# Tree attention on one core: SyncE's store of heads 88 and 90 in eleven pieces in place of four

## The chip, the core and the metric

The kernel runs on one core of a Trainium2 chip. Five engines work side by side: TensorE (PE, with its weight loads as PEld) multiplies matrices, VectorE (DVE), ScalarE (ACT) and GpSimd (POOL) work on tiles, and SyncE (SP) only issues transfers and waits. Sixteen DMA engines move data between the chip's memory (HBM) and the on-chip buffer. A transfer is issued by SP, ACT or POOL; the profile lists the packets of each issuer under a queue of its own: q1 is SP's, q10 ACT's, q0 POOL's.

The metric is the device time of one execution in microseconds. It is longer than the profile's span, which goes from the first instruction to the last.

## The reference

Q, K and V have 8 x 12 = 96 heads of 512 positions by 64 numbers, in fp32. The positions are the nodes of a binary tree, and a node attends to itself and to its ancestors:

```python
for i in range(seq):
    mask[i, i] = 1
    parent = i
    while parent > 0:
        parent = (parent - 1) // 2
        mask[i, parent] = 1
scores = np.einsum('bhqd,bhkd->bhqk', Q, K) * scale
scores = scores + (1 - mask) * (-1e9)
weights = np.exp(scores - np.max(scores, axis=-1, keepdims=True))
weights = weights / (np.sum(weights, axis=-1, keepdims=True) + 1e-10)
return np.einsum('bhqk,bhkd->bhqd', weights, V)
```

## The kernel before

The 96 heads are worked off as 48 pairs, `i` = 0 to 47 (`NP` = 48). For each pair the kernel transposes Q and K on TensorE (`narrow_k`, `wide_k` and their like, lines 401 and 433), makes the scores (`scores1`, `scores2`, lines 458 to 501; the mask enters as a product of small codes), takes their exponential on ScalarE (lines 476 and 507), multiplies by V (`values`, line 551) and divides by the sum that a column of ones in V gives (`norm`: a reciprocal on line 581 and a product on line 583, both on VectorE). From the ninth pair on the heads of a pair stand two apart: `head(i, a)` makes pair 44 out of heads 88 and 90, pair 45 out of 89 and 91, pair 46 out of 92 and 94, pair 47 out of 93 and 95.

The results lie in tiles of eight heads, one row of a tile for each of the 128 partitions; one row of one head is 1 KB. `store` (line 592) writes `n` heads, or the rows `p0` to `p1` of them, with one DMA. POOL issues nearly all loads and, eight heads at a time, the stores of heads 0 to 75 and 80 to 87, in the order that `pool_program` lists. SP issues two loads at the start, the store of heads 76 to 79 (`store_apart`), and then, from the loop's last three rounds and behind the loop, the stores of the last eight heads:

- in round 45 (`NP - 3`) heads 88 and 90, cut by rows at the places in `edges`: 4, 8, 12 and 104 rows,
- in round 46 heads 89 and 91, in round 47 heads 92 and 94, each in one DMA of 128 rows,
- behind the loop head 93; head 95 goes out from ACT.

An engine's instructions run in the order in which they are written, so SP issues these one after the other; each store waits for the product on line 583 that fills its tile. The framework also gives the DMAs of SP and ACT eight completion counters, one after another and then again from the first. A DMA that takes a counter for the second time first waits until the DMA that had the counter before has landed. In the kernel before, the store of 104 rows, those of heads 89 and 91, 92 and 94, and head 93 take the counters of the four loads at the start, and head 95's takes that of heads 76 to 79.

At the end SP waits for every counter (under line 792 in the profile, line 793 in the changed kernel), and a barrier over all engines closes the program.

Of the kernel before, what the change touches and what calls it, by code (L numbers as in the profile page):

```python
# [119 lines left out]
def kernel(  # L120
# [9 lines left out]
    P = nc.NUM_PARTITIONS  # L130
# [4 lines left out]
    NP = 2 * NQ  # L135
# [128 lines left out]
    def head(i, a):  # L264

        return 2 * i + a if i < WIDE else 4 * (i // 2) + i % 2 + 2 * a
# [178 lines left out]
    def turn(name, i):  # L445
        heads = [head(i + b, a) for b in range(2 if i >= WIDE else 1) for a in range(2)]
        assert all((name, h) in issued for h in heads), (name, i)
        {"kst": (narrow_k, wide_k), "qst": (narrow_q, wide_q)}[name][i >= WIDE](i)
        return i + (2 if i >= WIDE else 1)
# [4 lines left out]
    def scores1(i):  # L454

        sp = psS.tile([P, 2, 512], fp32, name="s1")
        for a in range(2):
            nc.tensor.matmul(  # L458
                out=sp[:, a, :],
                lhsT=(k1code if i < WIDE else k1wide)[64 * a:64 * a + CODE_ROWS, :],  # L460
                rhs=(q1code[64 * a:64 * a + CODE_ROWS, :] if i < WIDE
                     else q1wide[64 * a:64 * a + CODE_ROWS, :, :]),
                start=True, stop=False,
            )
        for a in range(2):
            nc.tensor.matmul(  # L466
                out=sp[:, a, :], lhsT=keys(i, a, TOP),
                rhs=qTs[i][64 * a:64 * a + 64, :, :].rearrange("p t c -> p (t c)"),
                start=False, stop=True,
            )  # L470
        et = etpool.tile([P, 2, 4, 128], bf16, name="e1")
        nc.scalar.activation(  # L472
            out=et[:, :, :, :].rearrange("p a t c -> p (a t c)"),
            in_=sp[:, :, :].rearrange("p a c -> p (a c)"),
            func=AF.Exp, scale=scale,
        ) if i < WIDE else nc.scalar.activation(  # L476
            out=et[:, :, :, :].rearrange("p a t (r u) -> p a (t r) u", u=2),
            in_=sp[:, :, :].rearrange("p a (u c) -> p a c u", u=2),
            func=AF.Exp, scale=scale,
        )  # L480
        ets[i] = et
# [31 lines left out]
    def scores2(i):  # L513
        if i >= WIDE:
            return scores2_wide(i)
        sp = psS.tile([P, 2, 4, 128], fp32, name="s2")
        flat = sp[:, :, :, :].rearrange("p a t c -> p a (t c)")
        for a in range(2):
            nc.tensor.matmul(
                out=sp[:, a, :, 32:128], lhsT=k2code[64 * a:64 * a + CODE_ROWS, :],  # L520
                rhs=q2code[64 * a:64 * a + CODE_ROWS, :].rearrange(
                    "p (t c) -> p t c", t=4
                )[:, :, 32:128],
                start=True, stop=False,
            )
        for t, lo, hi in ((2, 32, 192), (0, 192, 256), (3, 288, 448), (1, 448, 512)):
            for a in range(2):
                nc.tensor.matmul(
                    out=flat[:, a, lo:hi], lhsT=keys(i, a, TILE2[t]),
                    rhs=qTs[i][64 * a:64 * a + 64, :, :].rearrange("p t c -> p (t c)")[:, lo:hi],  # L530
                    start=False, stop=t == 1, skip_group_check=t in (2, 3),
                )
        nc.scalar.activation(
            out=e2s[i % NE][:, :, :, 32:128].rearrange("p a t c -> p (a t) c"),
            in_=sp[:, :, :, 32:128].rearrange("p a t c -> p (a t) c"),
            func=AF.Exp, scale=scale,
        )

    def values(i):

        if i < NP - 1:
            obs[i] = ob = psO.tile([P, 2, 512], fp32, name="ob")
        else:
            obs[i] = ob = psS.tile([P, 2, 512], fp32, name="s1")
        e1, e2, vt = ets[i], e2s[i % NE], vts[(head(i, 0) // VB) % NV]

        vtile = VTILE if i < WIDE else WVTILE
        assert all(("vt", n, head(i, a)) in issued for n in PARTS[i >= WIDE] for a in range(2))

        def product(e, a, t, tile_v, lo=0, hi=128, **flags):  # L550
            nc.tensor.matmul(  # L551
                out=ob[lo:hi, a, 65 * t:65 * t + 65],
                lhsT=e[:, a, PLACE[t], lo:hi],
                rhs=vt[vtile[tile_v][0]][:, head(i, a) % VB, vtile[tile_v][1], 0:D + 1],
                **flags,
            )

        def halves(a):
            for t in (0, 1):
                product(e2, a, t, 1 + SELF[t], 0, 64, start=False, stop=t == 1)  # L560
                product(e2, a, t, 1 + t, 64, 128, start=False, stop=t == 1)

        for a in range(2):
            for t in range(4):
                product(e1, a, t, 0, start=t == 0, stop=False)
            for t in (2, 3):
                product(e2, a, t, 1 + t, start=False, stop=False)
            if i == NP - 1:
                halves(a)
        if i < NP - 1:  # L570
            for a in range(2):
                halves(a)

    def norm(i):
        g = head(i, 0) // VO
        if g not in ofs:
            ofs[g] = opool.tile([P, VO, 4, D], fp32, name="of")
        o4 = obs[i][:, :, 0:260].rearrange("p a (t c) -> p a t c", c=D + 1)
        rec = small.tile([P, 2, 4, 1], fp32, name="rec")
        for a, n in ((0, 2),) if i < NP - 1 else ((0, 1), (1, 1)):  # L580
            nc.vector.reciprocal(out=rec[:, a:a + n, :, :], in_=o4[:, a:a + n, :, D:D + 1])  # L581
            first, last, step = head(i, a) % VO, head(i, a + n - 1) % VO, head(i, 1) - head(i, 0)
            nc.vector.tensor_tensor(  # L583
                out=ofs[g][:, first:last + 1:step, :, :],
                in0=o4[:, a:a + n, :, 0:D],
                in1=rec[:, a:a + n, :, :].to_broadcast([P, n, 4, D]),
                op=ALU.mult,
            )
# [8 lines left out]
        )  # L597

    APART, APART_AT = 76, 41

    def store_apart():

        store(nc.sync, APART, 4)
# [92 lines left out]
    def spread_by(copy, table, steady, i):  # L696

        o, j = divmod(i, 8)
        todo = table.get(i, [])
        if 4 <= o + 1 < NH // VB:  # L700
            todo = todo + [(o + 1,) + piece for piece in steady.get(j, [])]
        for args in todo:
            spread(copy, *args)
# [8 lines left out]
    def spin(name, n):  # L712

        pool, shape = (psS, [P, 2, 512]) if name == "s1" else (psO, [P, 2, 512])
        tile = pool.tile(shape, fp32, name=name)
        for _ in range(n):
            nc.tensor.matmul(
                out=tile[:, 0, :], lhsT=idle[:, 0:128], rhs=idle[:, :], start=True, stop=True
            )
# [9 lines left out]
    for i in range(NP + 1):  # L729
        steps = FIRST[i] if i < len(FIRST) else "SVK" if i % 2 else "SVQ"  # L730
        for step in steps:
            if step == "S" and i < NP:
                scores1(i)
                scores2(i)
            if step == "V" and i >= 1:
                values(i - 1)
                norm(i - 1)
                valued = True
            if step == "K" and kdone < NP:
                kdone = turn("kst", kdone)  # L740
            if step == "Q" and qdone < NP:
                qdone = turn("qst", qdone)
            if step == "W":
                nc.scalar.copy(
                    out=codes[64:64 + CODE_ROWS, 1280:1536], in_=codes[0:CODE_ROWS, 1280:1536]
                )
            if step == "X":
                spin("s1" if valued else "ob", 2)
            if step == "D":
                spread_by(nc.vector.tensor_copy, BY_VECTOR, STEADY_VECTOR, i)  # L750
            if step == "A":
                spread_by(nc.scalar.copy, BY_SCALAR, {}, i)
        if "D" not in steps:
            spread_by(nc.vector.tensor_copy, BY_VECTOR, STEADY_VECTOR, i)
        if "A" not in steps:
            spread_by(nc.scalar.copy, BY_SCALAR, {}, i)
        pool(i)
        if i == APART_AT:
            store_apart()
        if i >= NP - 3 and i < NP:  # L760
            edges = (0, 4, 12, 24, P) if i == NP - 3 else (0, P)
            for p0, p1 in zip(edges, edges[1:]):
                store(nc.sync, head(i - 1, 0), 2, 2, p0, p1)
    assert not program
# [32 lines left out]
```

## Time and profile before

| | |
|---|---|
| median of 3 runs | 134.81 us (134.7 to 135.66) |
| the profiled execution's own time | 135.35 us |
| its span | 133.6 us |
| outside the span | 1.75 us |
| busy: PE / DVE / ACT / POOL | 113.8 / 100.4 / 94.4 / 73.2 us |
| moved by DMA | 32.26 MB, 242 GB/s on average |
| packets on SP's queue (q1) | 1831, of 1.83 MB |

The page gives shares over the whole span. The change concerns the last 11 us of it, so the rows that count are those of short windows there: SP's issues in order of time with the time that each took, the packets of each queue in a window, and for a transfer the time from its issue to its landing. For DMAs that are split over fewer than sixteen engines the view has no time to landing.

### The profile page before, as it was taken

Reading aid. Unit: us, or ns where it says so; the run is one execution under the profiler, and the core shown is the slowest. Engines: PE = TensorE matmul, PEld = TensorE weight load, DVE = VectorE, ACT = ScalarE, POOL = GpSimd, SP = SyncE. Lnnn points to the kernel's source line nnn. Section 1 sums busy time; section 2 is a strip of 40 time slices with the busy share of each in tenths; the row PEclk is TensorE's granted clock in tenths of the full one; section 3 lists DMA queues with packets and bytes.
Section 4 is the critical chain, followed back from the end, with each engine's and each line's share of the span. In section 5 each row is a group of like instructions: output and inputs, shape, how many; then the busy total and the mean of one; then the engine's idle time right before and its main releaser. Section 6 shows DMA issues by size and latency. Waiting matters only on the chain.

```text
span 133.6 us, 5522 instructions
## 1 busy us (share of the span) xinstructions
PE 113.8 (85%) x2414; PEld 79.2 (59%) x2417; DVE 100.4 (75%) x249; ACT 94.4 (71%) x153; POOL 73.2 (55%) x100
## 2 busy tenths in 40 slices
PE   6884999999799899989989699969989997989800
PEld 2352676667577577756757468747657765756500
DVE  3437769998999998979796699977887896674620
ACT  4358289979769778868858769859785975959600
POOL 6978725364374999986932799538089510002000
PEclk9999599999999999999999999999999999999985
DMA  4999999999999999999999999999999999999981
GB/s 136 207 173 193 197 200 199 202 201 207 202 199 203 202 204 205 201 205 201 205 204 201 318 251 201 295 271 250 322 221 335 224 321 400 402 397 405 366 301 38
DMA packets 32239, 32.26 MB, mean 242 GB/s; under 512 B 1199, under 2 KB 29487, under 8 KB 32215
## 3 DMA queue, kind: packets, MB, share of 16 engines
q0 software_dynamic: 29824, 29.63, 113.8%
q1 hardware_dynamic: 1831, 1.83, 4.0%
q10 hardware_dynamic: 560, 0.46, 1.1%
q8 instruction: 19, 0.31, 0.9%
q14 instruction: 5, 0.04, 0.1%
HBM read 37.94 MB, written 12.58 MB: 378 GB/s over the span
## 4 chain that ended last, share of the span: by engine, by line
DMA 48%; PE 33%; issue 6%; POOL 5%; DVE 2%; ACT 2%; DVEq 0%; ACTq 0%; POOLq 0%
DMA vst<-in_V_dram 33%; PE ob L551 11%; DMA kst<-in_K_dram 10%; DMA qst<-in_Q_dram 6%; PE s L458 5%; PE qtp L433 3%; PE ktp L401 3%; PE s L466 3%; PE s L501 3%; PE s L491 3%; POOL kst L239 2%; POOL qst L239 2%; POOL vst L239 1%; DVE of L583 1%; ACT e L507 1%
## 5 line engine op out<-in xcount | busy, mean ns | idle before, releaser
L476 ACT ACTIVATE e<-s 128x1024 bf16<-128x1024 f32 x40 | 41.0, 1024 | 21.0 <-PE s L466 20.4
L551 PE MATMUL ob<-vt,e 128*128 128x65 bf16 (+1 forms) x940 | 37.8, 198 | 3.5 <-DVE of L583 2.1
L551 PEld LDWEIGHTS <-e 128*128 128x128 bf16 (+1 forms) x960 | 30.7, 103 | 11.9 <-DVE of L583 2.1
L507 ACT ACTIVATE e<-s 128x384 bf16<-128x384 f32 x80 | 34.7, 490 | 0.0
L583 DVE TENSOR_TENSOR of<-ob,rec 128x512 f32<-128x512 f32 x47 | 32.5, 691 | 1.6
L336 POOL COPY vt<-vst 32x512 int32<-32x512 int32 (+1 forms) x32 | 24.3, 759 | 8.1 <-DVE vt L336 5.0
L336 DVE COPY vt<-vst 64x1024 bf16<-64x1024 bf16 (+6 forms) x42 | 18.5, 440 | 3.8 <-DMA vst<-in_V_dram 3.1
L458 PE MATMUL s<-codes 40*128 40x512 bf16 x96 | 19.7, 398 | 1.2 <-issue 0.4
L581 DVE RECIPROCAL rec<-ob 128x8 f32<-128x8 f32 x47 | 9.6, 205 | 14.2 <-PE ob L551 13.5
L466 PE MATMUL s<-kq 64*128 64x512 bf16 x96 | 18.8, 382 | 0.0
L592 POOL DMA_DIRECT2D out_dram<-of x11 | 9.9, 900 | 15.7 <-DVE of L583 13.2
L280 POOL DMA_DIRECT2D vst<-in_V_dram x15 | 11.0, 736 | 12.2 <-DMA vst<-in_V_dram 5.2
L501 PEld LDWEIGHTS <-kq 64*128 64x128 bf16 x320 | 12.6, 94 | 4.8 <-issue 0.3
L501 PE MATMUL s<-kq 64*128 64x160 bf16 (+1 forms) x320 | 15.1, 208 | 0.2 <-issue 0.2
L401 PE MATMUL ktp<-ptile,kst 128*64 128x128 bf16 x320 | 12.5, 219 | 2.3 <-issue 2.0
L491 PE MATMUL s<-codes 40*128 40x384 bf16 x80 | 13.9, 334 | 0.3
L441 DVE COPY kq<-qtp 128x1024 bf16<-128x1024 bf16 x20 | 13.6, 681 | 0.6 <-PE qtp L433 0.6
L433 PE MATMUL qtp<-ptile,qst 128*64 128x128 bf16 x320 | 12.7, 219 | 1.2 <-issue 1.2
L472 ACT ACTIVATE e<-s 128x1024 bf16<-128x1024 f32 x8 | 8.2, 1023 | 6.0 <-PE s L466 6.0
L251 POOL DMA_DIRECT2D qst<-in_Q_dram x13 | 9.5, 730 | 4.6 <-DMA kst<-in_K_dram 1.5
L251 POOL DMA_DIRECT2D kst<-in_K_dram x12 | 8.9, 745 | 5.3 <-DMA kst<-in_K_dram 1.5
L491 PEld LDWEIGHTS <-codes 40*128 40x128 bf16 x80 | 6.3, 94 | 8.9 <-issue 1.3
(42 smaller groups left out, 121.4 us busy)
## 6 DMA issues: line engine op xcount, KB each, us to landing
out_dram<-of POOLq DMA_DIRECT2D x10, 1024.0 KB, 15.9
kst<-in_K_dram POOLq DMA_DIRECT2D x8, 512.0 KB, 14.9
qst<-in_Q_dram POOLq DMA_DIRECT2D x7, 512.0 KB, 16.6
vst<-in_V_dram POOLq DMA_DIRECT2D x12, 256.0 KB, 14.1
vst<-in_V_dram POOLq DMA_DIRECT2D x6, 512.0 KB, 12.7
qst<-in_Q_dram POOLq DMA_DIRECT2D x8, 256.0 KB, 11.5
kst<-in_K_dram POOLq DMA_DIRECT2D x6, 256.0 KB, 11.5
out_dram<-of POOLq DMA_DIRECT2D x1, 512.0 KB, 20.6
```

What stands on the lines that cost most here:

```text
L251: return nc.gpsimd.dma_start(out=kept[b][:, h0 % KB:h0 % KB + n, :, :].rearrange("p (g x) t d -> p g (x t d)", x=2), in_=wide[:, h0 // 2:( ...
L336: return copy(out=dst, in_=src)
L401: nc.tensor.transpose(out=columns(kp[64 * a:64 * a + 64, :], mixed, (256, 2), (leaves - mixed, 2), (1, 32)), in_=st[:, 2 * i % KB // 2 + a ...
L433: nc.tensor.transpose(out=halves[64 * a:64 * a + 64, :, c:c + 64], in_=st[:, 2 * i % KB // 2 + a, 4 * u + t, :], identity=ptile[:, 0:128],)
L458: nc.tensor.matmul(out=sp[:, a, :], lhsT=(k1code if i < WIDE else k1wide)[64 * a:64 * a + CODE_ROWS, :], rhs=(q1code[64 * a:64 * a + CODE_ ...
L466: nc.tensor.matmul(out=sp[:, a, :], lhsT=keys(i, a, TOP), rhs=qTs[i][64 * a:64 * a + 64, :, :].rearrange("p t c -> p (t c)"), start=False, ...
L476: ) if i < WIDE else nc.scalar.activation(
L491: nc.tensor.matmul(out=flat[:, a, :, :].rearrange("p u (t c) -> p u t c", t=4)[:, :, :, 16:64], lhsT=k2wide[64 * a:64 * a + CODE_ROWS, :], ...
L501: nc.tensor.matmul(out=flat[:, a, :, lo:hi], lhsT=keys(i, a, WTILE2[t]), rhs=qT[64 * a:64 * a + 64, :, lo:hi], start=False, stop=t == 1, s ...
L507: nc.scalar.activation(out=e2s[i % NE][:, a, :, 32:128].rearrange("p t (r u) -> p t r u", u=2), in_=flat[:, a, :, :].rearrange("p u (t r) ...
L551: nc.tensor.matmul(out=ob[lo:hi, a, 65 * t:65 * t + 65], lhsT=e[:, a, PLACE[t], lo:hi], rhs=vt[vtile[tile_v][0]][:, head(i, a) % VB, vtile ...
L583: nc.vector.tensor_tensor(out=ofs[g][:, first:last + 1:step, :, :], in0=o4[:, a:a + n, :, 0:D], in1=rec[:, a:a + n, :, :].to_broadcast([P, ...
```

## The change

The rows of heads 88 and 90 are cut at eleven places in place of four. The pieces have 5, 6, 7, 8, 9, 10, 11, 13, 14, 15 and 30 rows, which is 128 rows as before, of two heads each. Nothing else is edited.

```diff
     APART, APART_AT = 76, 41
+    LAST_ROWS = (0, 5, 11, 18, 26, 35, 45, 56, 69, 83, 98, P)
 
     def store_apart():
...
         if i >= NP - 3 and i < NP:
-            edges = (0, 4, 12, 24, P) if i == NP - 3 else (0, P)
+            edges = LAST_ROWS if i == NP - 3 else (0, P)
             for p0, p1 in zip(edges, edges[1:]):
                 store(nc.sync, head(i - 1, 0), 2, 2, p0, p1)
```

In the built program the instructions of PE, DVE, ACT and POOL stand as before. SP issues seventeen DMAs in place of ten. The counters fall otherwise: the pieces of 8, 9, 10 and 11 rows take those of the four loads at the start, the piece of 13 rows that of heads 76 to 79. From there on a store waits for another piece: 14 rows for the landing of the 6 rows, 15 for the 7, 30 for the 8, heads 89 and 91 for the 9 rows, heads 92 and 94 for the 10, head 93 for the 11, and head 95 on ACT for the 5. The pieces of 6 and 7 rows wait for nothing, as those of 8 and 12 rows did before.

## The prediction

> **What bounds the kernel now.** I began with the stretch that the change touches, the end of the program, and read the busy time of each engine there, two microseconds to a row. The columns are busy times with counts, then the granted clock, the share of the sixteen DMA engines in use, and GB/s.
>
> ```profile
> 122.00:124.00 2.00, 1.90 (x36) 1.26 (x37) 0.78 (x3) 1.84 (x4) 0.00 (x0) 1.00 1.02 391
> ...
> 126.00:128.00 2.00, 0.38 (x10) 0.21 (x7) 1.29 (x5) 0.00 (x0) 0.00 (x0) 1.00 1.02 368
> 128.00:130.00 2.00, 0.00 (x0) 0.00 (x0) 0.00 (x0) 0.00 (x0) 0.00 (x0) 0.87 0.79 275
> 130.00:132.00 2.00, 0.00 (x0) 0.00 (x0) 0.00 (x0) 0.00 (x0) 0.00 (x0) 0.50 0.23 80
> 132.00:134.00 2.00, 0.00 (x0) 0.00 (x0) 0.00 (x0) 0.00 (x0) 0.00 (x0) 0.50 0.00 0
> ```
>
> Until 128 all DMA engines are full. From 128 on nothing computes; only transfers run, and from 130 on only a quarter of the DMA engines: a few late ones finish by themselves. So the end is set by DMAs. To see whose, I took the issues of the end in order of time, and the time from issue to landing. The first three lines are VectorE finishing pair 44, VectorE finishing the last head, and ACT's store of it; the fourth is POOL's last store.
>
> ```profile
> 121.54 0.69 DVE L583 TENSOR_TENSOR of<-ob,rec 128x512 f32<-128x512 f32 x1
> 127.18 0.42 DVE L583 TENSOR_TENSOR of<-s,rec 128x256 f32<-128x256 f32 x1
> 127.64 0.35 ACTq L592 DMA_DIRECT2D out_dram<-of  x1
> 120.43 0.90 POOL L592 DMA_DIRECT2D out_dram<-of  x1 [13.23 <-DVE of L583]
> ...
> out_dram<-of POOLq DMA_DIRECT2D x1, 1024.0 KB, 9.4
> out_dram<-of SPq DMA_DIRECT2D x1, 256.0 KB, 5.7
> out_dram<-of SPq DMA_DIRECT2D x1, 256.0 KB, 5.5
> out_dram<-of ACTq DMA_DIRECT2D x1, 128.0 KB, 4.9
> ```
>
> ACT's store lands at 127.64 + 4.9 = 132.5, and the span of 133.6 ends 1.1 us later, with the final waits and the barrier. POOL's store of 1 MB, issued at 120.43, has its last byte down at 120.43 + 9.4 = 129.8. What does SP's queue do meanwhile? Queue rows of three windows:
>
> ```profile
> q0 software_dynamic: 309, 1.16, 100.3%
> q8 instruction: 1, 0.02, 2.1%
> ...
> q0 software_dynamic: 93, 0.36, 86.3%
> q1 hardware_dynamic: 16, 0.01, 5.1%
> ...
> q1 hardware_dynamic: 256, 0.25, 70.7%
> q0 software_dynamic: 31, 0.11, 27.1%
> ```
>
> The first two lines are 122 to 124.95: q1 has no row at all, though SP issued from 122.26 on. The next two are 124.95 to 126, the last two 127 to 128. So a store of SP waits on each DMA engine behind what POOL had queued there, and its packets run between 125 and the end. A packet of q1 takes 70.7% of 16 engine-microseconds over 256, or 44 ns; a store of 256 KB is 16 packets on each engine, 0.70 us, and one of 128 KB 0.35.
>
> **The change, part by part.** All of it is on SP. Its issues after 122, start and duration:
>
> ```profile
> 122.26 0.29 SPq L592 DMA_DIRECT2D out_dram<-of  x1
> 122.59 1.10 SPq L592 DMA_DIRECT2D out_dram<-of  x1
> 123.73 1.12 SPq L592 DMA_DIRECT2D out_dram<-of  x1
> 124.89 0.37 SPq L592 DMA_DIRECT2D out_dram<-of  x1
> 125.37 0.39 SPq L592 DMA_DIRECT2D out_dram<-of  x1
> 126.19 0.39 SPq L592 DMA_DIRECT2D out_dram<-of  x1
> 127.09 0.35 SPq L592 DMA_DIRECT2D out_dram<-of  x1
> ```
>
> In order these are the pieces of 4, 8, 12 and 104 rows, then heads 89/91, 92/94 and 93. Pair 44 is ready at 121.54 + 0.69 = 122.23, SP starts at once, and the four pieces hold SP until 125.26. The store of heads 89/91 starts only then.
>
> *How the pieces are spread.* The page's q1 row tells:
>
> ```profile
> q1 hardware_dynamic: 1831, 1.83, 4.0%
> ```
>
> If every DMA has one packet per row and head and one more for each DMA engine that it uses, the other stores and loads of SP come to 272 + 50 + 528 + 272 + 272 + 144 = 1538, which leaves 293 = 256 + 37 for heads 88/90, and 37 = 4 + 8 + 12 + 13. So 4, 8 and 12 rows go to as many engines, one row each, and 104 rows go to 13 engines, eight each. By the same count the new pieces use 5, 6, 7, 8, 9, 10, 11, 13, 14, 15 and 15 engines, together 113; ten pieces have one row per engine, the last has two. The Trainium skill ("DMA: Bandwidth & Descriptors", on why a DMA increments its semaphore by 16) states this rule, the largest number up to 16 that divides the rows, and adds that the lowest-numbered engines are taken; the first half agrees with the 1831 packets, the second no row here shows.
>
> *What it can gain.* An engine that ends late ends earlier by each row that it no longer gets. Before, none has more than 1 + 1 + 1 + 8 = 11 rows, 22 packets, so 22 x 44 ns = 0.97 us is the most that can go, and only if the latest engine had all and now gets none. By the skill's rule of lowest numbers the thirteenth engine goes from 8 rows to 5, 0.26 us, and the first four from 11 to 12.
>
> *What the issues cost.* Seven more DMAs on SP, each at between 0.29 and 1.12 us plus 0.04 to the next (122.59 + 1.10 to 123.73). Which end? The pieces with several rows per engine took 0.37 to 0.39. Of the three with one row per engine two took 1.10 and 1.12, the first 0.29, but that one had stood waiting for VectorE for a long time. The extra is equal in both, so it does not look like a queue's chance delay, and the 104 rows behind them were fast under the same load. The nearest rows to the pieces of 6 to 15 rows are therefore those two, and I take 1.15 us from start to start for nine pieces (6, 7, 8, 9, 10, 11, 13, 14, 15), 0.33 for the first and 0.48 for the 30 rows (124.89 to 125.37). The other bound is 0.41 for all.
>
> *The sum.* Pieces start at 122.26 and 122.59; nine at 1.15 bring the 30 rows to 132.94, heads 89/91 to 133.42, 92/94 to 133.90 and head 93 to 134.38, in place of 127.09. The new waits for counters are met long before, since everything that a piece queues behind is down at 129.8. The DMA engines are then empty, so part of the delay is got back: no queue, only the transfer's own latency. For this the nearest row is a 256 KB load at the program's start, with little else in flight, which landed 3.0 us after its issue:
>
> ```profile
> firstK<-in_K_dram SPq DMA_DIRECT2D x1, 256.0 KB, 3.0
> ```
>
> Less its 0.70 of packets that is 2.3 us beside the packets, an upper bound, as three other loads ran with it. The lower bound is what ACT's store shows: issued at 127.64, no q10 row before 128, so at least 0.4. I take 1.3. The 40 packets of the three stores then end at 133.42 + 1.3 + 40 x 0.044 = 136.5, where 132.5 was: **4.0 us later**. Nothing covers this, since no engine computes after 127.6; POOL's stores, compute and ACT's store are as before or earlier. The profiled execution's 135.35 becomes 139.35; it lies 0.54 above the median, so on the runs' median 134.81 the forecast is **138.8**. With 0.4 and 2.3 for the latency it is 137.9 to 139.8.
>
> **The rivals.**
>
> *The high price belongs to something else, and the time stays.* What speaks for it: the first piece at 0.29 had one row per engine too, and the pieces at 1.10 and 1.12 are the only ones here that wait for no counter or engine. If that is the condition, only 6 and 7 rows pay; if it is a state that ended near 125, when q1's first packets ran, likewise. Then 8 rows start at 124.89 as the 104 did, and 13 rows are out by 124.89 + 5 x 0.41 = 126.9. Now the counters bind: 89/91 waits for the landing of the 9 rows, between 125 (first packets) and 129.8 (POOL's last byte). Taking 129, the end is 129 + 1.3 + 1.76 = 132.1; the latest engine, with POOL's work until 129.8, five rows and 40 packets, also comes to 129.8 + 0.4 + 1.8 = 132.0. Against 132.5 that is -0.4 to, with a landing at 129.8, +0.4: 134.4 to 135.2, most likely 134.8. [...] The rows of 0.29 and 0.35 to 0.39 fit one price, 1.10 and 1.12 do not.
>
> *The high price lasts only while the DMA engines are full.* Their share falls to 0.79 after 128. Then 6 to 10 rows pay 1.15 each, until 128.34, the pieces of 11, 13, 14 and 15 cost 0.41, and 30 rows start at 129.98, 89/91 at 130.46. The end is 130.46 + 3.06 = 133.5, or 1.0 later; with one or two more dear pieces 1.8 or 2.5. That is 135.8 to 137.3.
>
> *Not slower but faster.* The mechanism is the late engines: their rows of heads 88/90 go to engines that are done before. The place is 130 to 132.5, the price 0.044 per packet, and it decides only if 89/91 is issued before POOL's packets on the late engines end at 129.8. It gives -0.26 by the count above, 134.5, and at most -0.97, 133.8, less than 1% even then.
>
> **How the numbers follow.** Forecast (price by shape) 0.43; price only in part of the stretch 0.17; time stays 0.35; late engines relieved 0.05. Changes under 1%, 1.35 us, can hardly be told from none in runs that spread by nearly 1 us. The forecast and nearly all of the second rival are slower by more than that; the last two are within 1%, but for the tails: faster 0.04, same 0.35, slower 0.61. The range must reach from the unchanged case to the forecast's upper bound, 134.3 to 139.8; the likeliest case alone is 137.9 to 139.8.
>
> **What the profile of the changed kernel would show.** SP's issues one by one: nine of 1.1 us, the last at 134.4, prove the price by shape; two of 1.1 and the rest near 0.37, with a gap on SP ahead of the stores of 14 rows and of 89/91, prove the first rival. q1 should count 1831 + 76 = 1907 packets. Between 129 and 134 the DMA share should fall near zero ahead of three last stores; if it doesn't, SP wasn't what they waited for. The forecast is wrong if a small piece with a wait already met is issued in 0.37 us.

## The result, and the profile after

The changed kernel takes 135.82 us (median of 13 runs, 135.53 to 136.17) where the kernel before takes 134.97 (median of 13 runs beside them, 134.55 to 136.0). The ratio is 1.0057, with a 95% interval of 1.0034 to 1.0080: slower by 0.6%, some 0.8 us, where 4.0 us were forecast. The ratios here and below compare the fast runs of the two kernels, so they need not be the quotient of the medians beside them.

SP's issues from 122 on, in the timeline of the changed kernel (start, duration); the first eight are the pieces of 5, 6, 7, 8, 9, 10, 11 and 13 rows, then come 14, 15 and 30 rows, heads 89/91, 92/94 and 93:

```profile
122.23 0.30 SPq L592 DMA_DIRECT2D out_dram<-of  x1
122.57 1.09 SPq L592 DMA_DIRECT2D out_dram<-of  x1
123.71 0.46 SPq L592 DMA_DIRECT2D out_dram<-of  x1
124.21 0.30 SPq L592 DMA_DIRECT2D out_dram<-of  x1
124.56 0.29 SPq L592 DMA_DIRECT2D out_dram<-of  x1
124.90 0.32 SPq L592 DMA_DIRECT2D out_dram<-of  x1
125.26 0.35 SPq L592 DMA_DIRECT2D out_dram<-of  x1
125.66 0.35 SPq L592 DMA_DIRECT2D out_dram<-of  x1
127.83 0.32 SPq L592 DMA_DIRECT2D out_dram<-of  x1
128.30 1.18 SPq L592 DMA_DIRECT2D out_dram<-of  x1
129.53 0.41 SPq L592 DMA_DIRECT2D out_dram<-of  x1
130.05 0.39 SPq L592 DMA_DIRECT2D out_dram<-of  x1
130.54 0.41 SPq L592 DMA_DIRECT2D out_dram<-of  x1
131.04 0.45 SPq L592 DMA_DIRECT2D out_dram<-of  x1
```

Eight pieces are out by 126.0, not by 130.6. Then SP stands until 127.83. What it waits for is in the view of the waits, from 121 to 134:

```profile
SPq L592 <- DVE of L583: 12.0, 1, 12.0
SPq L592 <- DMA out_dram<-of: 1.8, 1, 1.8
```

The second line is new: 1.8 us in which a store of SP waits for the landing of another store. By the built order it is the piece of 14 rows, which takes the counter of the piece of 6. Before, SP's stores waited for nothing but VectorE. Heads 89/91, which were out at 125.37, go out at 130.05. The busy table of the end (same columns as in the prediction) shows what that does to the transfers, and the page's q1 row how many packets they were:

```profile
124.00:126.00 2.00, 1.94 (x46) 1.46 (x42) 1.08 (x3) 1.78 (x3) 0.00 (x0) 1.00 0.97 375
126.00:128.00 2.00, 0.35 (x10) 0.18 (x6) 1.26 (x5) 0.00 (x0) 0.00 (x0) 1.00 0.63 238
128.00:130.00 2.00, 0.00 (x0) 0.00 (x0) 0.00 (x0) 0.00 (x0) 0.00 (x0) 1.00 0.39 121
130.00:132.00 2.00, 0.00 (x0) 0.00 (x0) 0.00 (x0) 0.00 (x0) 0.00 (x0) 0.63 0.70 235
132.00:134.00 2.00, 0.00 (x0) 0.00 (x0) 0.00 (x0) 0.00 (x0) 0.00 (x0) 0.50 0.39 137
...
q1 hardware_dynamic: 1907, 1.83, 4.0%
```

Between 126 and 130 the DMA engines, which were full or at 0.79 before, stand at 0.63 and 0.39; after 130, where they stood at 0.23 and 0.00, they now run at 0.70 and 0.39. The last three stores, 640 KB, have moved behind a gap. The span grows from 133.6 to 134.4.

### The profile page after: what moved, and what is told of

The parts are those of the page before. It is cut to its first block, busy times and chain, and to the rows that moved or that the text cites. A ratio compares the mean times of both kernels' runs of the same rounds, so it can differ in the third digit from the quotient of the medians.

```text
span 134.4 us, 5529 instructions
## 1 busy us (share of the span) xinstructions
PE 113.5 (84%) x2414; PEld 79.2 (59%) x2417; DVE 99.9 (74%) x249; ACT 94.4 (70%) x153; POOL 73.0 (54%) x100
## 3 DMA queue, kind: packets, MB, share of 16 engines
q1 hardware_dynamic: 1907, 1.83, 4.0%
## 4 chain that ended last, share of the span: by engine, by line
DMA 57%; PE 25%; issue 5%; POOL 5%; ACT 2%; DVE 1%; ACTq 0%; POOLq 0%
DMA vst<-in_V_dram 37%; DMA qst<-in_Q_dram 13%; PE ob L551 7%; DMA kst<-in_K_dram 7%; PE s L458 4%; PE s L466 3%; PE qtp L433 3%; PE ktp L401 2%; POOL vt L336 2%; PE s L501 2%; PE s L491 2%; POOL kst L251 1%; ACT e L507 1%; ACT e L472 1%; PE s L551 1%
## 5 line engine op out<-in xcount | busy, mean ns | idle before, releaser
L336 DVE COPY vt<-vst 64x1024 bf16<-64x1024 bf16 (+6 forms) x42 | 17.8, 425 | 6.6 <-DMA vst<-in_V_dram 6.0
L433 PE MATMUL qtp<-ptile,qst 128*64 128x128 bf16 x320 | 13.2, 224 | 1.3 <-issue 0.7
```

The source lines that it names most:

```text
L336: return copy(out=dst, in_=src)
L433: nc.tensor.transpose(out=halves[64 * a:64 * a + 64, :, c:c + 64], in_=st[:, 2 * i % KB // 2 + a, 4 * u + t, :], identity=ptile[:, 0:128],)
```

## The experiments

Two theories for the 0.8 us. **Counters**: heads 89/91 are held back by counters whose DMAs have not landed, until their transfers no longer fit beside the late DMA engines' own work. **Pieces**: seven more DMAs cost by their number, on SP or on the DMA engines. Beside them two questions from the prediction: whose the price of 1.1 us is, and whether relieving the late engines is worth anything.

### Eight pieces, and who waits for whom

```diff
-    LAST_ROWS = (0, 5, 11, 18, 26, 35, 45, 56, 69, 83, 98, P)
+    LAST_ROWS = (0, 5, 11, 18, 26, 35, 45, 56, P)
```

> Eight pieces: 5, 6, 7, 8, 9, 10, 11 and 72 rows. The first seven are those of the changed kernel, the last four are one. Heads 89/91 now wait for the landing of the 6 rows (127.8 in the changed kernel's trace) and not, behind three more waiting pieces, until 130.05. Theory of the counters: 89/91 starts at 127.9, before POOL's last packets are down on the late DMA engines, which then set the end as before: 134.6 to 135.2, within 0.4 us of the kernel before. Rival, the loss grows with the number of pieces (issues on SP, packets on the DMA engines): four more pieces of seven cost 4/7 of the change's 0.77 us, 0.44 us, 135.4.

135.34 us, ratio 1.0029 (1.0007 to 1.0052). That is 0.14 us above the range of the counters and 0.06 under the figure of the rival, so by the time alone the rival fits better. Its issue of heads 89/91, from the timeline:

```profile
128.02 0.39 SPq L592 DMA_DIRECT2D out_dram<-of  x1
```

Two microseconds earlier than with eleven pieces, with a span of 133.5 against the 133.6 before. But the profiled execution of the kernel before, 135.35 us, was itself 0.4 us above its median, and that of the eight pieces, 135.3, was not. So the early start does not explain why the eight pieces lose 0.4 us by their median; this part stays open.

### The three stores on POOL, with four and with eleven pieces

```diff
-                store(nc.sync, head(i - 1, 0), 2, 2, p0, p1)
+                store(nc.sync if i == NP - 3 else nc.gpsimd, head(i - 1, 0), 2, 2, p0, p1)
-    store(nc.sync, head(NP - 1, 0), 1)
+    store(nc.gpsimd, head(NP - 1, 0), 1)
```

> The kernel before, with heads 89/91, 92/94 and 93 stored by POOL and not by SP. POOL is free after 121.3; an issue there takes 0.9 us in place of 0.39. Both theories: within 1 us of the kernel before, since POOL's queue is drained first in, first out. It is the partner of the next run.

> Eleven pieces on SP as in the changed kernel, but heads 89/91, 92/94 and 93 stored by POOL, whose counters are others, so no store of theirs waits for a piece. Theory of the counters: no loss against its partner with four pieces, -0.4 to +0.3 us. Rival of the pieces themselves (their number, their packets, the load on the first DMA engines): the same 0.8 us over its partner as the change has over the kernel before.

135.36 us with four pieces (1.0024, 1.0000 to 1.0048) and 135.33 with eleven (1.0023, 1.0002 to 1.0045). Against the same kernel with four pieces the eleven cost nothing once the three stores do not stand behind them; both kernels are some 0.4 us slower than the kernel before. The heads 89/91 go out from POOL as soon as VectorE is done, in the trace with four pieces and in that with eleven:

```profile
124.99 0.71 POOL L592 DMA_DIRECT2D out_dram<-of  x1 [3.31 <-DVE of L583]
```

```profile
124.00 0.71 POOL L592 DMA_DIRECT2D out_dram<-of  x1 [3.31 <-DVE of L583]
```

Both are 2.4 us behind SP's first piece, which went out at 122.61 in the one execution and at 121.61 in the other. In the second run SP has eleven pieces with their dear issues and counter waits, its last one at 128.8, and the median time is the same:

```profile
127.17 0.32 SPq L592 DMA_DIRECT2D out_dram<-of  x1
127.80 0.99 SPq L592 DMA_DIRECT2D out_dram<-of  x1
128.83 0.41 SPq L592 DMA_DIRECT2D out_dram<-of  x1
```

So it is neither the number of pieces nor their packets nor SP's own issue time that costs by itself; it is that three stores stand behind them on SP.

### Four pieces of 32 rows

```diff
-    LAST_ROWS = (0, 5, 11, 18, 26, 35, 45, 56, 69, 83, 98, P)
+    LAST_ROWS = (0, 32, 64, 96, P)
```

> Four pieces of 32 rows, two rows for each of sixteen DMA engines, in place of 4, 8, 12 and 104. For the price of an issue: if 1.1 us belongs to pieces with one row per engine, all four issues take 0.29 to 0.4; if it belongs to the DMA that SP issues second after it stood waiting, the second takes 1.1 us again and the third between 0.4 and 1.1. The late DMA engines get eight rows as before, the last three of the sixteen get eight in place of none: within 0.4 us of the kernel before.

135.16 us, ratio 1.0019 (0.9994 to 1.0044). The four issues:

```profile
122.22 0.35 SPq L592 DMA_DIRECT2D out_dram<-of  x1
122.61 1.41 SPq L592 DMA_DIRECT2D out_dram<-of  x1
124.06 0.45 SPq L592 DMA_DIRECT2D out_dram<-of  x1
124.56 0.43 SPq L592 DMA_DIRECT2D out_dram<-of  x1
```

All four have the same shape and two rows per engine, and the second takes 1.41 us, the others 0.35 to 0.45. The price is not the shape's.

### Two pieces, and one

```diff
-    LAST_ROWS = (0, 5, 11, 18, 26, 35, 45, 56, 69, 83, 98, P)
+    LAST_ROWS = (0, 9, P)
```

> Heads 88/90 in two pieces, 9 and 119 rows: by the rule that fits the packet counts these use 9 and 7 DMA engines, so the late engines that had eight or nine rows before get none or one. Theory of the late engines (the only thing that the cut of the rows can improve): eight rows are 16 packets of 44 ns, the end comes 0.7 us earlier, 134.3 us. Rival, the late engines' share does not set the end: within 0.3 us of the kernel before.

135.43 us, ratio 1.0031 (1.0005 to 1.0056): not earlier. Its first two issues settle the shape once more, since the second has seventeen rows per engine by the packet rule:

```profile
121.84 0.32 SPq L592 DMA_DIRECT2D out_dram<-of  x1
122.20 1.06 SPq L592 DMA_DIRECT2D out_dram<-of  x1
```

The same cut for heads 89/91 as well:

```diff
-            edges = LAST_ROWS if i == NP - 3 else (0, P)
+            edges = LAST_ROWS if i < NP - 1 else (0, P)
```

> As the run with 9 and 119 rows, and heads 89/91 and 92/94 cut in the same way where no counter binds (88/90 and 89/91 in this kernel). Theory of the late engines: sixteen rows less on each late engine, 1.4 us, of which the first seven engines, which then have 36 rows in place of 18, give back some: the end comes 1.0 to 1.4 us earlier, 133.6 to 134.0 us. Rival: within 0.3 us of the kernel before, or later, as the first engines become the late ones.

135.93 us (twelve runs from 135.34 to 138.28), ratio 1.0063 (1.0032 to 1.0093): slower, as the rival had it. And heads 88/90 in one DMA, `LAST_ROWS = (0, P)`:

> Heads 88/90 in one DMA of 128 rows on all sixteen engines. Theory of the late engines: eight rows on each, as the late ones had before, within 0.3 us of the kernel before. Rival, small pieces on the first engines are what keeps the end early: 0.4 us or more slower than before.

135.38 us beside 135.17 for the kernel before, ratio 1.0015 (0.9996 to 1.0035): no difference that can be told. So no cut of these rows that was tried, into one, two, four even, eight, ten or eleven pieces, is faster than 4, 8, 12 and 104, and sparing the late engines, the one gain that the prediction allowed for, was not seen in any median. The profiled run with two pieces has a short span, 132.7, but the runs of that kernel range from 134.48 to 136.09, so that one trace says little.

### Ten pieces

```diff
-    LAST_ROWS = (0, 5, 11, 18, 26, 35, 45, 56, 69, 83, 98, P)
+    LAST_ROWS = (0, 5, 11, 18, 26, 35, 45, 56, 69, 83, P)
```

> Ten pieces: the last two of the eleven, 15 and 30 rows, are one of 45. The piece of 14 rows still waits for the 6 rows, the 45 rows wait for the 7, heads 89/91 for the 8. Theory of the counters with the dear second issue: 14 rows go out at 127.8, the 45 rows behind it take 1.1 to 1.2 us, heads 89/91 start near 129.6, 0.4 us before the changed kernel's 130.05; 0.3 to 0.5 us slower than before, 135.3 to 135.5. If the dear issue belongs to one row per engine, the 45 rows (three per engine) take 0.4, 89/91 starts at 128.8 and the time is that of before.

135.26 us beside 135.17, ratio 1.0000 (0.9977 to 1.0023): less than the 0.3 to 0.5 us expected. The pieces of 14 and 45 rows, and heads 89/91:

```profile
128.36 0.32 SPq L592 DMA_DIRECT2D out_dram<-of  x1
128.94 0.33 SPq L592 DMA_DIRECT2D out_dram<-of  x1
129.57 0.39 SPq L592 DMA_DIRECT2D out_dram<-of  x1
```

Heads 89/91 start at 129.57 as expected, but by another road: the 45 rows are second behind a piece that had waited and take only 0.33. There is a gap ahead of them (128.36 + 0.32 = 128.68 to 128.94), so they waited for a landing themselves. That is no rule either. With the three stores on POOL the 15 rows waited for 0.3 us in the same place (127.17 + 0.32 = 127.49 to 127.80) and took 0.99. In the first run with eight pieces heads 92/94 were second behind a store that had waited for 1.5 us, did not wait themselves, and took 0.41:

```profile
128.51 0.41 SPq L592 DMA_DIRECT2D out_dram<-of  x1
```

The profiled execution here, 135.69 us, is the longest of the ten runs, so its late start need not be that of the median run.

### The same eight sizes in another order, and eleven once more

Sizes 5, 72, 6, 7, 8, 9, 10, 11, measured side by side with the eight pieces and with the changed kernel, unedited:

```diff
-    LAST_ROWS = (0, 5, 11, 18, 26, 35, 45, 56, 69, 83, 98, P)
+    LAST_ROWS = (0, 5, 77, 83, 90, 98, 107, 117, P)
```

> The same eight sizes as in the run with eight pieces, in another order: 5, 72, 6, 7, 8, 9, 10, 11. Nothing changes but which piece has the counter that heads 89/91 wait for: the 72 rows on twelve DMA engines, whose landing waits for the late ones (130.2 in the run with eight pieces), in place of the 6 rows (127.9). Theory of the counters: heads 89/91 start at 130.2, and as the last landing came 3.15 us after that start both in the changed kernel (130.05 to 133.2) and with ten pieces (129.57 to 132.7), the last landing is at 133.4 and the time 0.7 to 1.1 us above the run with eight pieces of this call, 136.1 to 136.5. Rival, the number of pieces or of packets: the same time as with eight pieces, within 0.3 us.

> The eight pieces once more, as the partner of the other order in the same call. Both theories: as measured, 0.1 to 0.7 us above the kernel before; heads 89/91 start at 128.0.

> The changed kernel once more, to stand beside the eight pieces in the same call. Theory of the counters: heads 89/91 start between 129.8 and 130.2, 0.5 to 0.9 us slower than the kernel before and 0.3 to 0.6 us slower than eight pieces. Rival of the number of pieces: also slower than eight, and slower than the other order of eight.

The medians are 135.98 for the other order (1.0058, 1.0026 to 1.0090), 135.64 for the eight (1.0036, 1.0007 to 1.0065) and 135.81 for the eleven (1.0037, 1.0010 to 1.0064), beside 135.04 for the kernel before. The order goes the way that the counters ask for, but by 0.34 us, less than the 0.7 forecast, and the intervals overlap; eleven and eight, 0.3 to 0.6 us apart by the forecast, can't be told apart here. The traces are clearer. The wait of a store for a landing, from 121 to 134, with 72 rows in second place and then with 6:

```profile
SPq L592 <- DMA out_dram<-of: 3.5, 1, 3.5
```

```profile
SPq L592 <- DMA out_dram<-of: 2.1, 1, 2.1
```

and the issue of heads 89/91 in the other order, in the eight, and in the second trace of the eleven:

```profile
129.68 0.39 SPq L592 DMA_DIRECT2D out_dram<-of  x1
```

```profile
127.82 0.39 SPq L592 DMA_DIRECT2D out_dram<-of  x1
```

```profile
129.08 0.39 SPq L592 DMA_DIRECT2D out_dram<-of  x1
```

Between the other order and the eight nothing but the order of the pieces differs, and this start moves by 1.9 us (0.07 of it lies ahead of the pieces, as SP's first one went out at 122.03 and 121.96), the span from 133.4 to 134.1. The 129.08 of the eleven misses its forecast, 129.8 to 130.2, because that whole execution was early: SP's first piece went out at 121.18, and 89/91 follows 7.9 us behind it, as in the first trace (122.23 and 130.05, 7.8 us).

### Eleven in the reverse order

The strongest dose: the wide pieces first, so that the late pieces and heads 89/91 wait for those that land on the late engines.

```diff
-    LAST_ROWS = (0, 5, 11, 18, 26, 35, 45, 56, 69, 83, 98, P)
+    LAST_ROWS = (0, 30, 45, 59, 72, 83, 93, 102, 110, 117, 123, P)
```

> The eleven sizes of the changed kernel in the reverse order: 30, 15, 14, 13, 11, 10, 9, 8, 7, 6, 5. The pieces that the counters make others wait for are now the wide ones, which land only after the late DMA engines: 7 rows wait for the 15, 6 for the 14, 5 for the 13, heads 89/91 for the 11, 92/94 for the 10. Theory of the counters: the 7 rows go out at 130.0, the 6 behind them at 130.4, perhaps with a dear issue of 1.1 us, the 5 rows at 130.7 to 131.5, heads 89/91 at 131.1 to 131.9; the last landing comes 3.15 us later, at 134.2 to 135.1, and the time is 1.8 to 2.6 us above the kernel before, 136.8 to 137.6. Rival of the number of pieces, their packets or their issues: as the changed kernel, 0.5 to 0.9 us above the kernel before.

136.40 us beside 134.95, ratio 1.0099 (1.0067 to 1.0131): 1.45 us slower than before with the same eleven sizes. That lies between the 0.5 to 0.9 of the rival and the 1.8 to 2.6 of the counters, a little nearer to the counters. The landings came earlier than forecast, so the 7 rows went out at 128.82 and not at 130.0, and the last three pieces cost 0.26 to 0.28 each, none of them dear. The lines are SP's second issue, then its 7, 6 and 5 rows and heads 89/91, and its waits for landings from 121 to 134:

```profile
123.16 1.40 SPq L592 DMA_DIRECT2D out_dram<-of  x1
...
128.82 0.28 SPq L592 DMA_DIRECT2D out_dram<-of  x1
129.39 0.27 SPq L592 DMA_DIRECT2D out_dram<-of  x1
129.79 0.26 SPq L592 DMA_DIRECT2D out_dram<-of  x1
130.17 0.39 SPq L592 DMA_DIRECT2D out_dram<-of  x1
...
SPq L592 <- DMA out_dram<-of: 2.1, 2, 1.8
```

In these traces heads 89/91 start only 0.1 us later than in the changed kernel (130.17 against 130.05), and the spans are 134.5 and 134.4. That the reverse order costs 0.6 us more than the change, 136.40 against 135.82, rests on the medians of two sets of runs that were not taken side by side.

### What the traces have in common

Start of SP's first piece, start of heads 89/91 on SP, and the end of the span, for every kernel in which SP stores these heads behind a counter:

| kernel | first piece | start of 89/91 | span | span less start of 89/91 |
|---|---|---|---|---|
| eight pieces, again | 121.96 | 127.82 | 133.4 | 5.6 |
| eight pieces | 122.77 | 128.02 | 133.5 | 5.5 |
| eleven, again | 121.18 | 129.08 | 133.4 | 4.3 |
| ten | 122.77 | 129.57 | 133.9 | 4.3 |
| eight, other order | 122.03 | 129.68 | 134.1 | 4.4 |
| eleven (the change) | 122.23 | 130.05 | 134.4 | 4.35 |
| eleven, reversed | 122.75 | 130.17 | 134.5 | 4.3 |

From 129.08 on the span ends 4.3 to 4.4 us after this start: the three stores are the path to the end. For an earlier start the span stays at 133.4 to 133.5, near the 133.6 of the kernel before with its start at 125.37: something else ends there. The share of the DMA engines in use, in tenths and in 40 slices from 127.5 to 131.9, shows it for the eight pieces (again): after the full stretch one to three tenths run on from 130.7 to 131.6, the late DMA engines.

```profile
DMA  5942324897359999983599999999832121211000
```

An estimate from these rows: in its own trace the kernel before could start heads 89/91 as late as 133.6 - 4.35 = 129.25, so it has 3.9 us to spare. The change spends 4.7 of them, and the 0.8 beyond is what the span grew by. Of the 4.7 us, 0.7 are the longer issue of the first eight pieces (3.78 us in place of 3.11), 1.8 the wait for the 6 rows, and 2.2 the issue of the three pieces behind it (127.83 to 130.05). By this estimate neither the issues alone (2.9) nor the wait alone (1.8) would have used up the 3.9; the two together did.

Whoever compares medians has to know that the kernel before ranges over 1.5 us from run to run, and that its fastest run, 134.55, is 1 us under the fastest of the changed one, 135.53, while their slowest are alike (136.0 and 136.17). What makes its longer runs long was not looked into. A trace is one run of these: that of the changed kernel is the second longest of its 13, those of the eight and the eleven measured again are the second shortest of their twelve. And the medians of kernels in which heads 89/91 go out early lie above that of the kernel before as well, though hardly clear of noise: four pieces of 32 rows and the single piece by 0.2 us, four pieces with the three stores on POOL by 0.4. Why, and whether a part of the 0.8 us has the same cause, no run shows.

## Why the prediction was right and wrong

**What bounds the end** was right: transfers alone from 128 on, first POOL's backlog, then a few late engines. Nothing ahead of 122 changed.

**How the pieces are spread** was right: 1907 packets on q1, as counted.

**What the issues cost** is the step that failed. It took 1.15 us from start to start for nine pieces, from the rows of 1.10 and 1.12, because these had one row per engine. Of the nine, two took 1.09 and 1.18, the other seven between 0.29 and 0.46. The seven of them up to the 13 rows, forecast at 8.05 us, came to 3.4 (122.57 to 126.01); after that it was no longer a sum of issues alone, but a wait and then three more. The run with 32 rows apiece showed the price on a shape that was said to be free of it, and only in the second issue. So the sum put the 30 rows' start at 132.94, and it was 129.53. The prediction had noticed the odd one out, the first piece at 0.29 with one row per engine, and explained it away by its wait, without giving the same allowance to the 104 rows.

**The new waits for counters are met long before**: wrong, as a consequence. The sum put this term at nothing, which held only if SP were as slow as assumed. With quick issues SP reaches the counters before the DMAs that own them have landed, and it waits for 1.8 us.

**The first rival** named the mechanism: quick issues, then the counters bind, with a gap ahead of the 14 rows. These were seen; the second gap that it asked for, ahead of 89/91, was not (129.53 + 0.41 = 129.94 to 130.05), and the high price fell on the 6 and the 15 rows, not on the 6 and the 7. Its size was off too. It set heads 89/91 at 129, from the landing of the 9 rows, and ended within 0.4 us of the kernel before; measured were 130.05 and 0.8 us. What it left out was the chain ahead of 89/91: the 14 rows wait until 127.83, the 15 rows behind them take 1.18, the 30 rows follow. Its estimate of the tail was good, with some luck, as the 1.3 was chosen between 0.4 and 2.3: 1.3 + 1.76 = 3.06 us from the start of 89/91 to the last landing, and 1.1 more to the span's end, make 4.2 where 4.3 to 4.4 were measured.

**The second rival** (price only while the engines are full) falls: from 124.2 to 126.0, with the engines at 0.97, five pieces cost 0.29 to 0.35 each, and 1.18 us was paid at 128.3, in a stretch at 0.39.

**The late engines relieved**: no median showed it. The two pieces, of 9 and 119 rows, came out at 135.43. That they spare the late engines rests on the lowest-numbered engines being taken, which no row here shows.

The largest chance, 0.61, stood on slower by over 1%; the change is slower by 0.6%, which the prediction counted with the cases that can hardly be told from none.

## What to carry to other kernels

Count the completion counters before cutting a transfer: the DMA that takes a counter again waits for the landing of the one before, and everything behind it in the issuing queue waits too, however cheap the issue is. When SP's issues are read for a price, look at what each one stood behind as well as at its shape; two equal rows out of four are not yet a rule. And a store has slack only up to a certain start: find that point (here near 129, an estimate from traces that end at 133.4 to 133.6) before pricing a delay.

## What the runs showed of the hardware

- SP's issue of one of these stores took 0.26 to 0.46 us in most cases. In every trace in which a second piece of heads 88/90 directly followed the first, that second issue took 0.8 to 1.4 us, whatever its rows: 1.06 us (119 rows), 1.09 (6 rows), 1.40 (15 rows), 1.41 (32 rows). The third took between 0.29 (7 rows, eight pieces) and 1.12 (12 rows, before). Behind a wait for a landing the second took between 0.27 (6 rows, reverse order) and 1.18 (15 rows, the change). What SP does in the long ones no view shows, and their cause stays open.
- One thing stands beside many of the long ones. In the changed kernel's trace a packet of 16 KB on q8, the queue of the kind "instruction", begins at 122.4 and another at 128.1; the first took 1.0 us (2.1% of 16 engines over 2.95 us, below). The issues of 1.09 at 122.57 and of 1.18 at 128.30 both begin 0.2 us behind such a start. In the kernel before a packet of q8 begins at 122.5 and takes 1.0 us too; the issue of 1.10 at 122.59 falls into it, but that of 1.12 at 123.73 begins after its end. Whether the two are connected no run tested.
- A store of SP issued at 122.2 has no packet in q1 before 125, while POOL's queue takes all of the sixteen engines' time, before and after the change; in the changed kernel's window from 122 to 124.95 the queues are

```profile
q0 software_dynamic: 301, 1.16, 100.2%
q8 instruction: 1, 0.02, 2.1%
```

- The last 640 KB, in three stores issued half a microsecond apart, need 4.3 to 4.4 us from the first issue to the end of the span, five times over within 0.1 us.
